# Held-back weight loads, own tiles for w_o_a, an earlier first product, and another planned order in a tuned transformer layer on one Trainium2 core

## The chip, the core and the metric

The kernel runs on one NeuronCore of a Trainium2 chip. Its engines are TensorE (PE in the profile; PEld is its weight load), VectorE (DVE), ScalarE (ACT), GpSimd (POOL) and SyncE (SP). SP issues most DMAs; POOL and ACT can issue some too. The engines run side by side, each through its own list of instructions in order, and wait for each other by semaphores. The metric is the device time of one launch in microseconds. The kernel before took 2119.3 us (median of three runs, 2118.64 to 2120.64).

## The reference

One layer of a decoder trunk on x of 1024 tokens by 1024, all in float32:

```python
x = x + 0.5 * swiglu(rms_norm(x, g_ffn1), w1_gate, w1_up, w1_down)      # hidden 2816
h = rms_norm(x, g_mix)
(c_q, k_a, v_a, k_idx, w_idx, q_b, k_b, v_b, gate_a, gate_b) = split(h @ w_in)
c_q = rms_norm(c_q, g_cq)                                               # 1024 x 256, the "latents"
q_a   = rope(rms_norm(c_q @ w_uq_a, g_q_a));  q_idx = rope(c_q @ w_q_idx)
score = sum over heads of relu(q_idx . k_idx) * w_idx                   # causal; best 256 keys per query
y_a = softmax attention over the selected keys, then w_uv_a             # 1024 x 512
y_b = stick-breaking attention of q_b, k_b, v_b                         # 1024 x 512
merged = sigmoid(gate_a) * (y_a @ w_o_a) + sigmoid(gate_b) * (y_b @ w_o_b)
x = x + merged @ w_out
x = x + 0.5 * swiglu(rms_norm(x, g_ffn2), w2_gate, w2_up, w2_down)
```

## The kernel before

**Precision.** A float32 operand is split into a high part (ACT copies it to fp32r, a matmul type) and a low part (DVE or POOL subtracts the high part). A product is three matmuls, high by high, high by low and low by high. `split` (L297) does this for weights: a load on SP into a raw tile ("woa2r"), the high part on ACT ("woa2h"), the low part on POOL ("woa2l"). Tiles come from pools with a fixed number of buffers. A tile's load waits until the readers of the one that it replaces are done.

**Stages, in order of time.** The first FFN runs until some 656 us. Its gate and up products (`ffn_in`) use a scheme of seven products on 2 x 2 blocks: A11 to A22 are blocks of weights, B11 to B22 blocks of the normed and transposed x, S and T sums of them. At the start the four x tiles are read, ACT sums their squares, POOL takes the root, `norm` (L435) writes both halves of a normed tile on DVE ("ay"), PE transposes it ("pst"), and `turn` (L441) turns the transposes into B's high parts (ACT) and low parts (DVE). The first product is that of A11 and B11 ("pg"). What `ffn_in` makes goes to DRAM ("staged"). `ffn_out` (L715) reads it back ("aS49r", "aA127r") with the down weights ("aw", "ab") in four passes n of eleven steps p, twelve matmuls "p" each.

From some 656 to 1361 us come the projections and both attentions. Their first part makes c_q's rows: `latent_rows` normalizes them ("cqn" from "pscq", L846), POOL stores them to DRAM ("cqd", L1038), and `latents` (L1549) loads them back and PE transposes them ("pscqt", L1562). In this phase the order of PE, DVE, ACT and POOL is fixed by a planner, the class `Weave` (L97). Its parts are generators that name the engine and the tiles they need next; it keeps an estimated clock for each engine, takes the step that can start first, and records it. `cost` estimates an instruction. `flush` (L141) adds it to the clock, with a random factor of 3% either way drawn from a seed (`luck`), and reckons a DMA that POOL or ACT issues at 0.55 or 0.37 us, a constant of 2.4 us and the bytes at 250 GB/s. SP's order comes from the surrounding tile framework.

In this phase: "psdot" are the index scores' dots, "relu" their evacuation by ACT (L1742), "u" the weighted sum on DVE (L1749); "psf" are projections with a high part "evh" (ACT), a low part "evl" (DVE), or, for the gates, "evg" (ACT), which POOL stores in "gd" (L1249) from a ring of three tiles; "qx" and "qy" are turned by PE in "psqt" (L1715); "psz" are stick-breaking logits, "left" their evacuation; "pso" is the attention's sum over values, "yt" its evacuation, "psoa" the first half of y_a @ w_o_a (weights "oa0" to "oa6"), merged with the gates and stored in "md".

From 1361 us on comes the second half of y_a @ w_o_a ("psm", weights "woa0" to "woa6"), which DVE and ACT merge with the gates (loads "gate<-gd", "gate<-obd") into "m". Then comes w_out ("psout", weights "wout000" and so on), and the second FFN with the same functions as the first, until 2118 us. `ring` (L849) gives that stage its tiles for operands and for raw weights, each from two pools in turn. woa0 and woa2 are already fetched while the planner still runs.

The functions that the change touches:

## Time and profile before

| | before |
|---|---|
| median of the runs | 2119.3 us (2118.64 to 2120.64) |
| profiled execution, its own time | 2119.98 us |
| its span | 2118.2 us |
| PE busy | 2099.0 us (99%), 10196 matmuls |
| DVE, ACT, POOL busy | 72%, 50%, 43% |
| DMA | 387.79 MB, mean 183 GB/s |
| granted PE clock | 0.999 |

The page of the profile gives each engine's busy time, and the chain of work that ended last, followed back from the last instruction. A row of a timeline is: start, duration, engine, line of the kernel, operation, output<-input, shape, count; in square brackets the idle time of that engine before it, and what ended it. A row of the waits is: the waiting engine, line and tile, what it waited for, total, number and longest. A row of the DMA view ends with the count, the size of one and the median from issue to landing. A row of the windows is: window and length, busy time and count for PE, PEld, DVE, ACT and POOL, clock, DMA share, GB/s. All are in us.

### The profile page before, as it was taken

What the parts mean: (1) busy time and instruction counts of PE and PEld (TensorE: products, weight loads), DVE (VectorE), ACT (ScalarE), POOL (GpSimd) and SP (SyncE); (2) the same over time, 40 slices, a digit from 0 to 9 for tenths busy, and PEclk for the clock granted to TensorE, in tenths of its full rate; (3) what the DMA queues carried; (4) which work ended last, traced back from release to release, by engine and by line L of the source; (5) the groups of instructions that cost most, each with busy time, mean ns of one, the idle gap of its engine ahead of it and who ended that gap; (6) DMA issues with size and microseconds to landing.
All of it is one profiled execution on the core that took longest, in us unless ns stands there. A gap on an engine that the chain in (4) does not pass through costs nothing.

```text
span 2118.2 us, 29830 instructions
## 1 busy us (share of the span) xinstructions
PE 2099.0 (99%) x10196; PEld 1762.7 (83%) x10196; DVE 1520.3 (72%) x2483; ACT 1058.0 (50%) x1992; POOL 911.2 (43%) x727
## 2 busy tenths in 40 slices
PE   9999999999999999999999999999999999999999
PEld 7888888888889978888888888878888888888887
DVE  7866767678875599788896688865756556487675
ACT  6343343334445356788896687535432322324443
POOL 6654555532336334431213342355655545542233
PEclk9999999999999999999999999999999999999999
DMA  5577777497685253586647754764143333359655
GB/s 150 158 249 220 244 205 236 155 326 255 208 228 159 74 162 110 207 225 171 178 158 232 257 174 157 239 230 157 46 125 100 105 98 126 95 189 335 217 174 189
DMA packets 298104, 387.79 MB, mean 183 GB/s; under 512 B 40144, under 2 KB 186224, under 8 KB 297952
## 3 DMA queue, kind: packets, MB, share of 16 engines
q1 hardware_dynamic: 285088, 343.90, 52.4%
q0 software_dynamic: 12864, 41.99, 5.4%
q8 instruction: 80, 1.31, 0.3%
q14 instruction: 72, 0.59, 0.1%
HBM read 264.67 MB, written 121.15 MB: 182 GB/s over the span
## 4 chain that ended last, share of the span: by engine, by line
PE 90%; DVE 3%; issue 2%; DMA 2%; ACT 2%; POOL 1%; SPq 0%; POOLq 0%; ACTq 0%; DVEq 0%
PE p L778 7%; PE p L779 7%; PE p L777 6%; PE pd L540 4%; PE pd L538 4%; PE pc L538 4%; PE pd L539 4%; PE pa L540 4%; PE pa L538 4%; PE pa L539 3%; PE pc L540 3%; PE pc L539 3%; PE psf L316 3%; PE psf L317 3%; PE psf L318 3%
## 5 line engine op out<-in xcount | busy, mean ns | idle before, releaser
L1390 ACT ACTIVATE junka<-u,cand,sig 128x1024 bf16<-128x1024 f32 (+3 forms) x124 | 134.2, 1082 | 5.7 <-DVE cand L1382 3.7
L1836 DVE TENSOR_TENSOR_SCAN left<-left,hidden 128x640 f32<-128x640 f32 (+3 forms) x64 | 89.1, 1411 | 1.6 <-ACT left L1830 1.4
L901 ACT ACTIVATE swh<-swr 128x512 fp32r<-128x512 f32 x48 | 30.2, 630 | 117.1 <-issue 52.2
L902 DVE TENSOR_TENSOR swr<-swr,swh 128x512 f32<-128x512 f32 x48 | 42.4, 884 | 39.6 <-ACT swh L901 36.9
L1890 DVE SCALAR_TENSOR_TENSOR pt<-pstT,pt 128x512 fp32r<-128x512 f32 (+1 forms) x96 | 51.5, 548 | 18.3 <-ACT pt L1887 17.6
L681 ACT ACTIVATE b0u<-b0u 128x512 f32<-128x512 f32 x20 | 12.6, 632 | 99.8 <-DVE b0u L561 84.4
L1249 POOL DMA_DIRECT2D gd<-evg x32 | 17.9, 560 | 86.8 <-ACT evg L1244 61.5
L1742 ACT ACTIVATE relu<-psdot 128x512 f32<-128x512 f32 (+1 forms) x80 | 40.4, 523 | 29.7 <-DVE u L1749 20.2
L1887 ACT ACTIVATE pt<-pstT 128x512 fp32r<-128x512 f32 (+1 forms) x96 | 46.4, 495 | 17.5 <-PE pstT L1962 14.8
L778 PE MATMUL p<-aT,aS 128*128 128x512 f32 x132 | 51.5, 390 | 1.2 <-DVE aT L391 1.2
L778 PE MATMUL p<-bT,bS 128*128 128x512 f32 x132 | 51.4, 389 | 0.0
L1749 DVE SCALAR_TENSOR_TENSOR u<-relu,WI,u 128x512 f32<-128x512 f32 (+1 forms) x70 | 49.7, 731 | 2.3 <-ACT relu L1742 1.4
L779 PE MATMUL p<-aT,aS 128*128 128x512 f32 x132 | 50.8, 390 | 0.0
L779 PE MATMUL p<-bT,bS 128*128 128x512 f32 x132 | 50.7, 389 | 0.0
L777 PE MATMUL p<-bT,bS 128*128 128x512 f32 x132 | 47.0, 389 | 0.0
L1962 PE MATMUL pstT<-ident,left 128*128 128x128 f32 x288 | 46.0, 273 | 0.0
L2016 ACT ACTIVATE e<-e,mx 128x768 f32<-128x768 f32 (+7 forms) x54 | 41.0, 760 | 8.9 <-DVE mx L2007 8.6
L777 PE MATMUL p<-aT,aS 128*128 128x512 f32 x132 | 44.9, 389 | 0.0
L1830 ACT ACTIVATE left<-psz 128x512 f32<-128x512 f32 (+2 forms) x96 | 43.2, 501 | 2.5 <-PE psz L1855 2.4
L1962 PEld LDWEIGHTS pstT<-ident,left 128*128 128x128 f32 x288 | 35.8, 140 | 8.5
L390 ACT ACTIVATE bT<-bt 128x512 fp32r<-128x512 f32 x44 | 26.2, 624 | 31.8 <-PE p L779 27.6
L1386 DVE TENSOR_SCALAR_CACHE_REDUCE junkv<-u,cand 128x512 uint8<-128x512 f32 (+1 forms) x62 | 41.6, 671 | 0.5
(3065 smaller groups left out, 8130.1 us busy)
## 6 DMA issues: line engine op xcount, KB each, us to landing
aw<-in_w_down_dram SPq DMA_DIRECT2D x33, 512.0 KB, 5.0
bw<-in_w_down_dram SPq DMA_DIRECT2D x33, 512.0 KB, 5.1
swr<-in_w_in_dram SPq DMA_DIRECT2D x48, 256.0 KB, 6.0
a0r<-in_w_gate_dram SPq DMA_DIRECT2D x22, 512.0 KB, 7.9
a1r<-in_w_up_dram SPq DMA_DIRECT2D x22, 512.0 KB, 7.3
b0r<-in_w_gate_dram SPq DMA_DIRECT2D x22, 512.0 KB, 4.3
b1r<-in_w_up_dram SPq DMA_DIRECT2D x22, 512.0 KB, 3.9
x<-in_x_dram SPq DMA_DIRECT2D x16, 512.0 KB, 6.3
```

Source lines behind the costliest of these rows:

```text
L316: nc.tensor.matmul(ps, ah, bh, start=first, stop=False)
L317: nc.tensor.matmul(ps, ah, bl, start=False, stop=False)
L318: nc.tensor.matmul(ps, al, bh, start=False, stop=last)
L538: nc.tensor.matmul(ps, a[:, c], b[k][:, HI], start=start and k == 0, stop=False, skip_group_check=True)
L539: nc.tensor.matmul(ps, a[:, c], b[k][:, LO], start=False, stop=False, skip_group_check=True)
L540: ins = nc.tensor.matmul(ps, a[:, l], b[k][:, HI], start=False, stop=k == 3, skip_group_check=True)
L777: nc.tensor.matmul(ps[q][m], S[:, h], T[:, HI], start=p == 0, stop=False)
L778: nc.tensor.matmul(ps[q][m], S[:, h], T[:, LO], start=False, stop=False)
L779: nc.tensor.matmul(ps[q][m], S[:, l], T[:, HI], start=False, stop=p == last)
L1390: nc.scalar.activation(junks[1][:, 0:(i + 1) * P], score[i], AF.Sign, scale=sig[:, b:b + 1], bias=cand.bitcast(F32)[:, b:b + 1], accum_out ...
L1836: nc.vector.tensor_tensor_scan(back, back, ones, 1.0, op0=ALU.mult, op1=ALU.max)
L1962: nc.tensor.transpose(tp[:, q * P:(q + 1) * P], A[n + q][:, j * P:(j + 1) * P], ident)
```

## The change

1. The start of the first FFN: the second halves of the norms of x tiles 2 and 3 move from DVE to ACT (`norm(late)`, `rest`). The first product (A11 with B11) stands right behind B11's transposes, ahead of B21's, with its matmul on B's low part last in each group of three. The copy of the first raw bank (`also`) goes to the end of `turn`, and B21's banks are named in another order.
2. The loads of the weights for c_q ("wcq0", "wcq1") and for v_b ("wvb00", "wvb01") each wait for a product of the first FFN's last pass (`pace`, `late_in_tail`).
3. c_q's rows are stored by SP where POOL did it, and loaded back in two halves each.
4. The planner reckons a store with a constant of 3.4 us in place of 2.4, and draws its factors from another seed.
5. w_o_a's remaining parts take tiles of the last stage's own pool, and that stage's raw tiles come from its own pool first.

```diff
--- before.py
+++ after.py
@@ -110,7 +110,7 @@
         self.ready, self.done, self.base = defaultdict(float), defaultdict(float), defaultdict(float)
         self.by, self.held, self.marks = {}, defaultdict(int), {}
         self.streams, self.own, self.last = [], None, 0.0
-        self.luck = random.Random(111)
+        self.luck = random.Random(96)
         self.cold, self.shared, self.sbuf, self.summed = 0, [], 0.0, False
 
     def cost(self, i, eng, outs, ins):
@@ -156,7 +156,7 @@
                     t, eng = self.free[SP] + 4.0, "DMA"
                 else:
                     t = max(t, self.free[eng]) + (0.55 if eng == POOL else 0.37)
-                    self.free[eng], t, eng = t, t + 2.4 + mb / 0.25, "DMA"
+                    self.free[eng], t, eng = t, t + 3.4 + mb / 0.25, "DMA"
             else:
                 cost, late = self.cost(i, eng, outs, ins)
                 cost *= self.luck.uniform(1 - 0.03, 1 + 0.03) if eng != PE else 1.0
@@ -294,11 +294,11 @@
         nc.gpsimd.tensor_tensor(rs, ms, mhalf[:, 0:n], op=ALU.pow)
         return rs
 
-    def split(src, nm, view, rawt=rawt, wt=wt):
+    def split(src, nm, view, rawt=rawt, wt=wt, pace=lambda i: i):
 
         raw = rawt(nm + "r")
         rv, n = view(raw)
-        nc.sync.dma_start(rv, src)
+        pace(nc.sync.dma_start(rv, src))
         wh = wt(nm + "h")
         nc.scalar.activation(wh[:, 0:n], raw[:, 0:n], AF.Copy)
         wl = wt(nm + "l")
@@ -402,7 +402,7 @@
         def __init__(self, g, bank, gains, yt, ct, tt, ts, spare, nm):
             self.g, self.bank, self.gains, self.yt, self.ct = g, bank, gains, yt, ct
             self.tt, self.ts, self.spare, self.nm = tt, ts, spare, nm
-            self.B, self.y, self.gcol = {}, {}, None
+            self.B, self.y, self.gcol, self.late = {}, {}, None, []
 
         def busy(self, n):
 
@@ -432,10 +432,17 @@
             nc.scalar.activation(j.bitcast(BF16), self.x[t], AF.Square, accum_out=ss)
             self.rs[t] = rsqrt(ss, 1, D)
 
-        def norm(self, t):
+        def norm(self, t, late=False):
             xt = self.x[t]
-            for c, out_ in ((slice(0, 1024), xt),) if self.half else ((HI, self.y[0, 0][t]), (LO, self.y[0, 1][t])):
+            for c, out_ in ((slice(0, 1024), xt),) if self.half else ((HI, self.y[0, 0][t]), (LO, self.y[0, 1][t]))[:1 if late else 2]:
                 nc.vector.tensor_scalar(out_, xt[:, c], self.rs[t], None, op0=ALU.mult)
+            if late:
+                self.late.append((self.y[0, 1][t], xt[:, LO], self.rs[t]))
+
+        def rest(self):
+
+            out_, x_, rs = self.late.pop(0)
+            nc.scalar.activation(out_, x_, AF.Copy, scale=rs)
 
         def operands(self, *ns):
             for n in ns:
@@ -457,11 +464,11 @@
                 t = self.B[n][k]
                 self.keep([(t[:, HI], ps)])
                 self.less([t[:, LO]], [ps], [f32(t[:, HI])])
-                if also is not None and not k:
-                    self.keep([(also, ps)], nc.vector)
                 if less:
                     self.less(less[0][k:k + 1], [ps], less[1][k:k + 1])
                 out.append(ps)
+            if also is not None:
+                self.keep([(also, out[0])], nc.vector)
             return out
 
         def keep(self, copies, eng=None):
@@ -532,12 +539,14 @@
 
             return rest if early else rest()
 
-        def times(a, b, ps, start=True):
+        def times(a, b, ps, start=True, low_last=False):
             for k in range(4):
                 c, l = slice(k * P, (k + 1) * P), slice(512 + k * P, 512 + (k + 1) * P)
-                nc.tensor.matmul(ps, a[:, c], b[k][:, HI], start=start and k == 0, stop=False, skip_group_check=True)
-                nc.tensor.matmul(ps, a[:, c], b[k][:, LO], start=False, stop=False, skip_group_check=True)
-                ins = nc.tensor.matmul(ps, a[:, l], b[k][:, HI], start=False, stop=k == 3, skip_group_check=True)
+                sides = [(a[:, c], b[k][:, HI]), (a[:, c], b[k][:, LO]), (a[:, l], b[k][:, HI])]
+                if low_last:
+                    sides[1:] = sides[:0:-1]
+                for n, (x_, y_) in enumerate(sides):
+                    ins = nc.tensor.matmul(ps, x_, y_, start=start and not k and not n, stop=k == 3 and n == 2, skip_group_check=True)
             return ins
 
         def mul(O, n, ps, start=True):
@@ -580,11 +589,11 @@
 
             ps, sg = {}, {}
 
-            def half(r, c, q, letter=None):
+            def half(r, c, q, letter=None, low_last=False):
 
                 if not q:
                     ps[r, c] = bank("pg", letter)
-                times(O[0][f"A{r + 1}{q + 1}"], B[f"B{q + 1}{c + 1}"], ps[r, c], not q)
+                times(O[0][f"A{r + 1}{q + 1}"], B[f"B{q + 1}{c + 1}"], ps[r, c], not q, low_last)
 
             def gate(r, c):
                 sg[r, c] = ct(f"{nm}sg")
@@ -596,11 +605,14 @@
 
             if "B11" not in B:
                 left(0, "A11")
+                R.rest()
                 R.operands("B12", "B11", "B21", "B22", "T1")
                 R.kept()
                 copies = list(zip(R.raw["T3"], R.turn("B11", between=6, also=R.raw["T3"][0])))
+                half(0, 0, 0, "a", True)
+                R.rest()
                 left(0, "A12")
-                p21 = R.turn("B21")
+                p21 = R.turn("B21", "bcda")
                 R.kept2()
                 copies += zip(R.raw["T4"], p21)
                 left(0, "A21", "A22")
@@ -623,7 +635,8 @@
             A[1].update(S)
             for t in rows:
                 R.norm(t)
-            half(0, 0, 0, "a")
+            if (0, 0) not in ps:
+                half(0, 0, 0, "a")
             half(0, 0, 1)
             gate(0, 0)
             left(1, "S2")
@@ -712,6 +725,8 @@
 
     STAGED = {n: i for i, n in enumerate(("A11", "A12", "A22", "S1", "S2", "S3", "S4"))}
 
+    product_of = {}
+
     def ffn_out(nm, xs, wd, raw, op, sums, aux, bank, staged, after):
 
 
@@ -776,7 +791,7 @@
                         h, l = slice(m * P, (m + 1) * P), slice(512 + m * P, 512 + (m + 1) * P)
                         nc.tensor.matmul(ps[q][m], S[:, h], T[:, HI], start=p == 0, stop=False)
                         nc.tensor.matmul(ps[q][m], S[:, h], T[:, LO], start=False, stop=False)
-                        nc.tensor.matmul(ps[q][m], S[:, l], T[:, HI], start=False, stop=p == last)
+                        product_of[nm, n, p] = nc.tensor.matmul(ps[q][m], S[:, l], T[:, HI], start=False, stop=p == last)
 
                 for _ in range(2):
                     if later:
@@ -846,10 +861,11 @@
         nc.vector.tensor_scalar(c, ps, rs, None, op0=ALU.mult)
 
 
-    def ring(pool):
+    def ring(pool, own=False):
 
         op = in_turn((wt, 4), (lambda name: pool.tile([P, 1024], F32R, tag="r", name=name, bufs=NR), NR))
-        raw = in_turn((rawt, 2), (lambda name: pool.tile([P, 1024], F32, tag="raw", name=name, bufs=2), 2))
+        raws = [(rawt, 2), (lambda name: pool.tile([P, 1024], F32, tag="raw", name=name, bufs=2), 2)]
+        raw = in_turn(*(raws[::-1] if own else raws))
         return op, raw
 
     def of(pool, tag, bufs, n=1024, dt=F32):
@@ -926,7 +942,7 @@
             for t in range(4):
                 if t < 3:
                     R.stat(t + 1)
-                R.norm(t)
+                R.norm(t, t > 1)
             R.second = lambda: R.place(xs[4:8], 1, sums)
             ffn_in("a", R, w1_gate, w1_up, raw, op, sums, ct, bank, staged[0], range(4), first, beside)
             assert not agenda and not held and not halved and not pieces
@@ -1019,9 +1035,12 @@
         aux = of(pool, "u", 8, 512)
         sums = in_turn((sums, 5), (lambda name: f32(pair(name)), 2))
         ffn_out("a", xs, w1_down, raw, op, sums, aux, bank, staged[0], after)
-        Wcq = [wcols(w_in, C_CQ, QR, 4 * j, 4, f"wcq{j}", rawt=raw,
+        def late_in_tail(p):
+            return lambda load: behind(product_of["a", 3, p], load)
+
+        Wcq = [wcols(w_in, C_CQ, QR, 4 * j, 4, f"wcq{j}", rawt=raw, pace=late_in_tail(j),
                      wt=lambda name: rpool.tile([P, 1024], F32R, tag="r", name=name, bufs=NR)) for j in range(2)]
-        Wvb = [wcols(w_in, C_VB, 256, 4 * j, 4, f"wvb0{j}") for j in range(2)]
+        Wvb = [wcols(w_in, C_VB, 256, 4 * j, 4, f"wvb0{j}", pace=late_in_tail(2 + j)) for j in range(2)]
 
         Rka, Rwi = [rawt(f"wka{j}r") for j in range(2)], cst.tile([P, 8 * ND], F32, name="wir")
         for j in range(2):
@@ -1035,7 +1054,7 @@
                 c = lat(f"cqn{half}{q}")
                 for j in range(2):
                     latents_normed(c[:, j * QR:(j + 1) * QR], banks_(q + j))
-                put_low(cqd[half][:, q * QR:(q + 2) * QR], c)
+                nc.sync.dma_start(cqd[half][:, q * QR:(q + 2) * QR], c)
 
         def one(q):
             ps = bank("pscq")[:, 0:QR]
@@ -1550,7 +1569,8 @@
 
             rows = [sring(f"cqn{half}") for half in range(2)]
             for half in (1, 0):
-                nc.sync.dma_start(rows[half], cqd[half])
+                for c in (slice(0, 512), slice(512, 1024)):
+                    nc.sync.dma_start(rows[half][:, c], cqd[half][:, c])
                 nc.sync.dma_start(*((rope, roped), (ropeq, ropeqd))[1 - half])
             for half in (1, 0):
                 cqn, outs = rows[half], []
@@ -2258,12 +2278,13 @@
 
 
     with ctxf, tc.tile_pool(name="ring2", bufs=1) as rpool, tc.tile_pool(name="ps6", bufs=1, space=PSUM) as psum:
-        op, raw = ring(rpool)
+        op, raw = ring(rpool, True)
         bank = banks(psum, fpsum)
         with tc.tile_pool(name="m0", bufs=1) as mpool:
             M0 = []
             for d in range(0, ND, 2):
-                wh, wl = first.pop(0) if first else wcols(w_o_a, d * P, 2 * P, 0, 4, f"woa{d}")
+                wh, wl = first.pop(0) if first else wcols(w_o_a, d * P, 2 * P, 0, 4, f"woa{d}",
+                                                              wt=lambda name: rpool.tile([P, 1024], F32R, tag="r", name=name, bufs=NR))
                 for e in range(2):
                     r = slice((d + e) * P, (d + e + 1) * P)
                     g = ht("gate", F32)
```

Where instructions move, the orders of the two kernels show it. First PE at the start: "pst" are transposes (of "ay" with numbers 244 to 247 for B11, 248 to 251 for B21), "pg" the first product. Before:

```order
L452 MATMUL pst_353<-ident_71,ay02_246 128x128
L452 MATMUL pst_353<-ident_71,ay03_247 128x128
L452 MATMUL pst_363<-ident_71,ay10_248 128x128
L452 MATMUL pst_363<-ident_71,ay11_249 128x128
```

...and twelve more transposes later:

```order
L452 MATMUL pst_384<-ident_71,ay13_251 128x128
L538 MATMUL pg_456<-aB110_293,a00A11_286 128x512
L539 MATMUL pg_456<-aB110_293,a00A11_286 128x512
```

Now:

```order
L459 MATMUL pst_351<-ident_71,ay02_246 128x128
L459 MATMUL pst_351<-ident_71,ay03_247 128x128
L549 MATMUL pg_359<-aB110_292,a00A11_284 128x512 x3
L549 MATMUL pg_359<-aB111_293,a00A11_284 128x512 x3
L549 MATMUL pg_359<-aB112_294,a00A11_284 128x512 x3
L549 MATMUL pg_359<-aB113_295,a00A11_284 128x512 x3
L459 MATMUL pst_376<-ident_71,ay10_248 128x128
L459 MATMUL pst_376<-ident_71,ay11_249 128x128
```

The first product stands behind the last of B11's transposes, and B21's sixteen follow it.

Second, ACT around the split of the weight wvb11 at some 822 us, in the planned part. Before:

```order
L1742 ACTIVATE relu<-psdot 128x384
L1742 ACTIVATE relu<-psdot 128x512
L1742 ACTIVATE relu<-psdot 128x384
L1128 ACTIVATE wvb11h<-wvb11r 128x1024
L1225 ACTIVATE evh<-psf 128x512
L1742 ACTIVATE relu<-psdot 128x512
L1742 ACTIVATE relu<-psdot 128x384
```

Now:

```order
L1762 ACTIVATE relu<-psdot 128x384
L1762 ACTIVATE relu<-psdot 128x512
L1762 ACTIVATE relu<-psdot 128x384
L1762 ACTIVATE relu<-psdot 128x512
L1147 ACTIVATE wvb11h<-wvb11r 128x1024
L1244 ACTIVATE evh<-psf 128x512
L1744 ACTIVATE qsa<-psqt 64x4x128
L1762 ACTIVATE relu<-psdot 128x384
L1762 ACTIVATE relu<-psdot 128x512
```

wvb11h still stands between relus, with evh behind it, and now a qsa as well.

Third, SP at the end of the attention, where the loads for the merged half stand ("gate" are the gates' rows and the stored products). Before:

```order
L1124 DMA woa2r<-in_w_o_a_dram 128x4x256
L2185 DMA both<-gd 128x512
L2188 DMA both<-obd 128x512
L2185 DMA both<-gd 128x512
L2188 DMA both<-obd 128x512
L301 DMA woa4r<-in_w_o_a_dram 128x4x256
L2270 DMA gate<-gd 128x512
L2271 DMA gate<-obd 128x512
```

Now, after ten other loads of "gate":

```order
L2291 DMA gate<-gd 128x512
L2292 DMA gate<-obd 128x512
L1143 DMA woa2r<-in_w_o_a_dram 128x4x256
L2291 DMA gate<-gd 128x512
L2292 DMA gate<-obd 128x512
L2291 DMA gate<-gd 128x512
L2292 DMA gate<-obd 128x512
L301 DMA woa4r<-in_w_o_a_dram 128x4x256
L301 DMA woa6r<-in_w_o_a_dram 128x4x256
L301 DMA wout000r<-in_w_out_dram 128x2x512
```

woa2r stood ahead of all loads of "gate", and stands behind twelve of the sixteen; the other weights stand behind all of them.

## The prediction

> **What bounds the kernel now.** I read the page first: busy time by engine, then the chain that ended last.
>
> ```profile
> PE 2099.0 (99%) x10196; PEld 1762.7 (83%) x10196; DVE 1520.3 (72%) x2483; ACT 1058.0 (50%) x1992; POOL 911.2 (43%) x727
> PE 90%; DVE 3%; issue 2%; DMA 2%; ACT 2%; POOL 1%; SPq 0%; POOLq 0%; ACTq 0%; DVEq 0%
> ```
>
> TensorE (PE) is busy in 2099.0 of 2118.2 us and is 90% of the chain. The change neither adds nor removes a matmul, so only PE's idle time can change. Where that lies, by stage (length after the colon, then PE's busy time and matmuls; the last columns are granted clock, DMA share, GB/s):
>
> ```profile
> 725.00:1361.00 636.00, 630.77 (x3393) 536.80 (x3391) 528.63 (x1175) 470.78 (x952) 208.38 (x250) 1.00 0.60 183
> 1361.00:1480.00 119.00, 116.51 (x523) 95.35 (x524) 69.06 (x80) 50.72 (x75) 59.10 (x32) 1.00 0.60 213
> 1480.00:2118.00 638.00, 633.56 (x2807) 523.86 (x2805) 411.56 (x522) 226.76 (x401) 293.40 (x198) 1.00 0.46 150
> ```
>
> The last stage gives a matmul's price: 633.56 / 2807 = 0.226 us. It also holds the tail after the last matmul, some 4 us, which the change leaves alone. The clock is full in all three. So the question is which of PE's waits go, and the waits of PE, summed by what ended them (us in total, times, longest), are the list to work through:
>
> ```profile
> PE psdot L1771 <- ACT relu L1742: 2.6, 4, 1.4
> PE psout L317 <- POOL wout000l L305: 1.2, 1, 1.2
> PE p L778 <- DVE aT L391: 1.2, 1, 1.2
> PE pscqt L1562 <- DMA cqn<-cqd: 1.2, 1, 1.2
> PE psf L316 <- ACT evg L1244: 1.2, 1, 1.2
> PE pst L452 <- ACT ay L432: 0.9, 1, 0.9
> PE pst L452 <- DVE ay L438: 0.8, 2, 0.7
> PE psqt L1715 <- POOL qx L1707: 0.7, 1, 0.7
> PE psz L1854 <- ACT left L1830: 0.6, 2, 0.3
> PE psm L316 <- DVE yt L1909: 0.6, 1, 0.6
> PE psm L318 <- POOL woa6l L305: 0.6, 1, 0.6
> PE psm L316 <- ACT woa2h L1128: 0.2, 1, 0.2
> ```
>
> These sum to 11.6 us, and each touches a part of the change. That is the ceiling of any gain here, 0.55%.
>
> **The start.** Two of the eight norm halves leave VectorE (DVE), and the first product moves ahead of B21's sixteen transposes. A row of DVE (tile 2) and one of ScalarE (ACT):
>
> ```profile
> 9.71 0.88 DVE L438 TENSOR_SCALAR ay<-x,rs 128x512 f32<-128x512 f32 x2 [0.66 <-POOL rs L294]
> 12.30 2.42 ACT L473 ACTIVATE aB<-pst,agcol 128x512 fp32r<-128x512 f32 x4 [0.81 <-PE pst L452]
> ```
>
> Only tiles 2 and 3 lose their second half (0.44 us each). Tile 2's comes off ahead of tile 3's statistic, so the last x tile is normed some 0.3 us sooner: a gain of 0.3 in the wait on ay (0.8). Against it stands the cover. Before, B21's sixteen transposes ran while ACT and DVE turned B11 into high and low parts. Now the product follows at once, and needs the first block's low part: ACT 0.6 (2.42 / 4) after the transposes, then one DVE step of 0.74 at most, against four blocks' transposes of about 0.4 each and two matmuls that don't read it. That leaves some 0.2 us of wait there, and some 0.4 at B21, whose transposes now end just ahead of their product. Sum +0.3. Bounds: -0.3 if all is hidden, +0.8 if each of the two waits lasts a whole ACT step.
>
> **Weight loads held back.** Here SyncE's queue (SP), the ACT step that waited, and PE:
>
> ```profile
> 595.27 0.38 SPq L301 DMA_DIRECT2D wcq0r<-in_w_in_dram  x1
> 600.78 1.14 SPq L301 DMA_DIRECT2D wcq1r<-in_w_in_dram  x1
> 602.01 0.53 SPq L722 DMA_DIRECT2D aS310r<-staged  x1
> 612.98 0.63 ACT L390 ACTIVATE aS<-aS310r 128x512 fp32r<-128x512 f32 x1 [6.41 <-DMA aS310r<-staged]
> 617.89 0.50 PE L778 MATMUL p<-aT,aS 128*128 128x512 f32 x1 [1.23 <-DVE aT L391]
> 648.16 1.07 ACT L303 ACTIVATE wcq0h<-wcq0r 128x1024 fp32r<-128x1024 f32 x1
> ```
>
> aS310r is 256 KB and took 11 us to land, issued right behind two 512 KB weight loads that aren't used for another 50 us. ACT stood 6.4 us for it, and PE then 1.23. With both loads gone from ahead of it, even half of those 6.4 us covers 1.23: -1.2. The loads move behind ab_5863, each after a product of the last pass (wcq0r first, wvb00r two places on). An estimate for wcq0r: its product ends 27 us (ten products of twelve matmuls) before the pass does at 656, so it goes out near 629, and even at aS310r's 11 us it lands 8 us ahead of its split at 648.16. Nothing that stands behind them on SP is wanted sooner than its own buffer comes free. Bounds: -1.2 and 0 (DMA contention has another source).
>
> **The latents' rows.** GpSimd (POOL) stored them and SP loaded them back:
>
> ```profile
> 685.91 0.54 POOL L1038 DMA_DIRECT2D cqd<-cqn  x1 [0.27 <-DVE cqn L846]
> 691.68 0.32 SPq L1553 DMA_DIRECT2D cqn<-cqd  x1
> 695.37 0.85 PE L1562 MATMUL pscqt<-ident,cqn 128*128 128x128 f32 x6 [1.19 <-DMA cqn<-cqd]
> staged<-b0u SPq DMA_DIRECT2D x20, 256.0 KB, 2.2
> x2d<-x SPq DMA_DIRECT2D x16, 256.0 KB, 3.7
> ```
>
> The path is store 5.8 us, load 3.7, wait 1.19. SP's stores of the same 256 KB land in 2.2 to 3.7, so 2.1 us or more come off against 1.19 to save: -1.2. SP now issues four stores and four half loads in place of two loads, six more of some 0.35 us. The pair of cqd0 waits for DVE at 685.6, and behind it stand only the rows themselves and weights issued after 691.68 before. Bounds: -1.2 and 0. [...]
>
> **The planner.** The scatter's seed and one us more for a listed store change no work, but they reorder all five engines from some 725 to 1361 us, where PE loses 2.6 + 1.2 + 0.7 + 0.6 = 5.1 us by the rows above. I went through those places in the new order:
>
> ```profile
> 822.03 1.06 ACT L1128 ACTIVATE wvb11h<-wvb11r 128x1024 fp32r<-128x1024 f32 x1 [1.61 <-PE psf L317]
> 808.00:826.00 18.00, 16.14 (x77) 13.04 (x75) 17.29 (x33) 10.43 (x21) 9.24 (x10) 1.00 0.34 118
> 1146.26 0.60 ACT L1244 ACTIVATE evg<-psf 128x512 f32<-128x512 f32 x1 [1.42 <-DMA gd<-evg]
> gd<-evg POOLq DMA_DIRECT2D x32, 256.0 KB, 5.0
> ```
>
> The longest wait on relu (1.4) comes of wvb11h: it waits on ACT for PE to leave the weight's slot, and the relus stand behind it. The new order keeps wvb11h behind four relus with evh behind it: 1.4 stays. Of the other relu waits (2.6 - 1.4 = 1.2) the later ones have some 0.7 us (three matmuls) more cover and go; 0.4 stays. psqt on qx gets four matmuls more (+0.9 of cover), and loses two list steps of DVE ahead of qy (1.0): 0.9. psz keeps its form: 0.6. The third evg stood 1.42 us on ACT until a gate store landed and freed its buffer; the planner now reckons 0.55 + 3.4 + 1.05 = 5.0 us for such a store, which is the row's median, where it took 4.0, and at one of the two places where it is close psf's pairs lie farther apart: 0.6 of 1.2 stays. Sum 3.9 of 5.1: -1.2. What I can't see is where the new order has a wait of its own, so this term is the wide one: -4 (four fifths of the 5.1 gone) to +3 (two more places like the worst two, 1.4 + 1.2, and a bit).
>
> **The merged half.** w_o_a's parts now come from the pool's own slots, so a split needn't wait for PE to leave an older one:
>
> ```profile
> 1353.54 0.50 SPq L2270 DMA_DIRECT2D gate<-gd  x1
> 1360.98 0.32 SPq L2271 DMA_DIRECT2D gate<-obd  x1
> 1359.91 1.06 ACT L1128 ACTIVATE woa2h<-woa2r 128x1024 fp32r<-128x1024 f32 x1 [0.54 <-issue]
> 1361.06 2.70 POOL L1133 TENSOR_TENSOR woa2l<-woa2r,woa2h 128x1024 fp32r<-128x1024 f32 x1 [2.40 <-ACT woa2h L1128]
> 1363.78 0.38 SPq L301 DMA_DIRECT2D woa6r<-in_w_o_a_dram  x1
> ```
>
> Before, PE lost 0.2 (woa2h) + 0.6 (yt) + 0.6 (woa6l) + 1.2 (wout000l) = 2.6. In the new order the attention's last matmuls lie ahead of 48 of psoa (10.8 us), so yt is early; and wout000 is split without waiting for woa's slots. But woa2r now stands behind twelve gate loads on SP. Those took 1353.54 to 1361.3, 7.8 us. Counted from psoa's 48, woa2h is wanted after 72 matmuls, 16.3 us, and its low part 0.9 later. The gate loads start a few us ahead of that count; woa2r goes out 6 to 8 us into it, lands 6 later, and with 1.06 and 2.70 is split at 16 to 18. woa6r waits for woa2l's end, and woa6h is wanted 6.3 us after woa2h. So 0 to 1 at each, and I take 0.9 in all for 2.6: -1.7. Bounds: -2.6 and +1.
>
> **The sum.** +0.3 - 1.2 - 1.2 - 1.2 - 1.7 = -5.0. The profiled execution took 2119.98 (1.8 beside its span of 2118.2), 0.7 above the median of 2119.3, so 2115.0 on its scale and **2114.3** on the median's.
>
> **Rivals.** Below, "same" is within 0.2% (4.2 us), about what a measurement of this kernel tells from no change.
>
> First, the new order's own waits eat the gain. For it: DVE was busy 17.29 of 18 us around 808 to 826, where two of the relu waits lie, so a few list steps put early make PE wait; against it: over the whole stage DVE has 107 us to spare. Planner term +3, total -0.8: 2118.5.
>
> Second, w_o_a comes late. SP's order speaks for it (a load behind twelve others); 10.8 us of psoa ahead of it speak against. If woa2r goes out 3 us later, woa2l and woa6h cost 3 in all in place of 0.9, and the start's +0.8 may join: 2117.
>
> Third, SP's store is as slow as POOL's, and the held loads were not what aS310r waited for: both terms 0, so 2116.7. Against it, the two loads stand right ahead of aS310r.
>
> Fourth, slower: DVE becomes the bound in the list stage. There the steps on relu take 0.73 each, against three matmuls' 0.68:
>
> ```profile
> L1749 DVE SCALAR_TENSOR_TENSOR u<-relu,WI,u 128x512 f32<-128x512 f32 (+1 forms) x70 | 49.7, 731 | 2.3 <-ACT relu L1742 1.4
> ```
>
> In one stretch of the new order, 38 matmuls (8.6 us) stand beside DVE steps that I count at 12.8; before, that stretch was even. If PE has no lead there, that place costs up to 4.2 us. With one such place the total is about zero (4.2 against the other terms' -3.8); it decides from the second on, 8.4 - 3.8 = +4.6, so 2123.9.
>
> Fifth, the planner's order happens to free most of the 5.1: term -4, 2111.5.
>
> **How the numbers follow.** The forecast 54% (its own range 2112 to 2116.5), the first rival 17%, the second 10%, the third 3%, the fourth 7%, the fifth 9%. The likeliest is 2114.3. Faster than 2115.1 are the fifth and most of the forecast's share (46 of 54): 55%. Slower than 2123.5 is the fourth: 7%. The rest, 38%, is within 0.2%. The range takes in the first three rivals and part of the fifth: 2110.5 to 2119.5.
>
> **What would show it.** In the profile after: no wait of p on aT near 618, and ACT's wait for aS310r under 3 us; cqd's stores landing in under 4 us and no wait of pscqt; at the start, pg waiting on aB for 0.2 and 0.4; wvb11h still ahead of a wait of psdot; no psm on yt, and a wait on woa2l or woa6h below 1 each. A PE sum between 725 and 1361 us more than 3 above 5.1, or any wait over 2 us there, would make the prediction wrong, and so would a matmul price other than 0.226.

## The result: slower by 0.69%

| | before | changed |
|---|---|---|
| median of six runs | 2119.97 us (2118.64 to 2120.85) | 2133.84 us (2132.49 to 2137.20) |
| ratio | | 1.0069, 95% interval 1.0056 to 1.0081 |
| profiled execution, its span | 2119.98, 2118.2 us | 2132.49, 2130.7 us |

The change cost 13.9 us, where a gain of 5.0 had been forecast. The profiled execution of the changed kernel is the fastest of its six. It has the same 10196 matmuls, and PE is again the chain. The largest waits of PE, summed by what ended them:

```profile
PE pst L363 <- DVE mlo L372: 5.5, 2, 4.6
PE psdot L1791 <- ACT relu L1762: 3.5, 4, 1.6
PE pst L459 <- ACT ay L432: 2.0, 2, 1.2
PE psm L316 <- ACT woa4h L303: 1.6, 1, 1.6
PE pa L549 <- DVE ar L478: 1.4, 1, 1.4
PE psz L1874 <- ACT left L1850: 1.4, 2, 1.0
...
PE psm L318 <- POOL woa2l L1152: 1.3, 1, 1.3
PE pscqt L1582 <- DMA cqn<-cqd: 1.1, 3, 0.5
...
PE psm L316 <- ACT woa2h L1147: 0.7, 1, 0.7
...
PE psm L318 <- POOL woa4l L305: 0.5, 1, 0.5
```

Of the waits that the change was to remove, those on aT (1.2), evg (1.2), qx (0.7), yt, woa6l and wout000l are gone. In their place stand others in the same stages, and the largest, 5.5 us on mlo (the low part of the normed and transposed rows that the projections use), had no counterpart before. Since PE's work is the same, the start of the matmul with a given number in PE's order, in the one trace less in the other, shows where the time went:

| matmuls | stage | the changed kernel falls behind by |
|---|---|---|
| up to 203 | start of the first FFN | 2.3 us |
| to 2854 | down products, place of the old wait on aT | -1.5 |
| to 2956 | end of the first FFN, 645 to 671 us | 9.0 |
| to 3466 | c_q's rows loaded back | 0.4 |
| to 7136 | planned stage and merged half | 2.5 |
| to the end | w_out, second FFN | -0.3 |

Before rounding, the rows sum to the 12.5 us between the two spans; the medians differ by 1.4 more.

**The largest piece.** SP's issues of the changed kernel, from its timeline, then the answers for three tiles (duration of the issue in ns, start; then the time from issue to landing in us):

```profile
630.09 0.38 SPq L301 DMA_DIRECT2D wcq0r<-in_w_in_dram  x1
630.57 0.46 SPq L1019 DMA_DIRECT2D xd<-x  x1
631.12 0.38 SPq L737 DMA_DIRECT2D aA127r<-staged  x1
631.59 0.43 SPq L301 DMA_DIRECT2D wcq1r<-in_w_in_dram  x1
632.12 2.08 SPq L775 DMA_DIRECT2D ab<-in_w_down_dram  x2
634.29 0.59 SPq L737 DMA_DIRECT2D aA128r<-staged  x1
634.97 0.56 SPq L301 DMA_DIRECT2D wvb00r<-in_w_in_dram  x1
...
L301 SPq DMA_DIRECT2D wcq0r<-in_w_in_dram x1: 384/384/384, 630.1 to 630.1; - x1
DMA to landing us min/median/max: 10.4/10.4/10.4
...
L737 SPq DMA_DIRECT2D aA127r<-staged x1: 382/382/382, 631.1 to 631.1; - x1
DMA to landing us min/median/max: 11.3/11.3/11.3
...
L737 SPq DMA_DIRECT2D aA128r<-staged x1: 593/593/593, 634.3 to 634.3; - x1
DMA to landing us min/median/max: 14.9/14.9/14.9
```

wcq0r landed at 640.5, and aA127r, half its size and issued 1 us later, at 642.4. SP's landings stand here in the order of issue: the last load ahead of wcq0r at 632.5, wcq0r 8.0 us after it, a store of x 1.3 after that, and then aA127r. aA128r behind wcq1r landed at 649.2; before it took 3.5 us. The same happened to aS310r near 602 us in the kernel before, which took 10.9; here there is less slack. Then ACT, and PE:

```profile
642.55 0.63 ACT L390 ACTIVATE aA<-aA127r 128x512 fp32r<-128x512 f32 x1 [9.42 <-DMA aA127r<-staged]
...
649.24 0.63 ACT L390 ACTIVATE aA<-aA128r 128x512 fp32r<-128x512 f32 x1 [0.65 <-DMA aA128r<-staged]
...
650.29 0.67 ACT L371 ACTIVATE mhi<-pst,gcolm 128x512 fp32r<-128x512 f32 x1
...
652.53 0.66 PE L363 MATMUL pst<-ident,m1xn 128*128 128x128 f32 x4 [4.60 <-DVE mlo L372]
655.39 0.63 PE L793 MATMUL p<-aB,aA 128*128 128x512 f32 x1
655.82 0.63 PE L794 MATMUL p<-aB,aA 128*128 128x512 f32 x1
...
640.00:650.00 10.00, 7.86 (x42) 6.10 (x40) 2.05 (x2) 2.54 (x5) 1.29 (x2) 1.00 0.98 240
650.00:656.00 6.00, 2.61 (x11) 2.18 (x12) 4.53 (x5) 4.96 (x9) 4.44 (x4) 0.76 0.15 56
656.00:662.00 6.00, 6.00 (x24) 4.80 (x23) 3.23 (x5) 3.71 (x6) 3.64 (x2) 0.67 0.46 69
```

In ACT's list the evacuation of the transposed m1xn (650.29) stands behind aA127r and aA128r (642.55 and 649.24), and PE stood 4.6 us for it (mlo is what DVE makes of mhi). Then the windows' clock column falls to 0.76 and 0.67: a matmul's step is 0.43 us (655.39 to 655.82), and 0.23 again from 661.13 to 661.36. Of the row's 9.0 us, 5.5 are waits, 2.8 were lost from 654.05 to 660.03 with the clock at half, and 0.7 at restarts and a short stop ahead of them.

**The start.** Here the product of the up weights waits for DVE, which copies B21's transposes out of PSUM:

```profile
24.68 0.74 DVE L478 TENSOR_SCALAR ar<-pst,agcol 128x512 f32<-128x512 f32 x1
...
25.57 2.99 PE L549 MATMUL pa<-aB,a10A 128*128 128x512 f32 x12 [1.36 <-DVE ar L478]
```

Of the 2.3 us, 1.6 come up here, with the restart. The longer waits on ay cost little: where the first product begins, the changed kernel is 0.2 behind, and ahead of the place above 0.7.

**c_q's rows.** SP's stores were issued at 695.42 behind wqir, and the loads that need them at 702.24; the wait of pscqt went from 1.2 to 1.1 in all:

```profile
694.89 0.43 SPq L1143 DMA_DIRECT2D wqir<-in_w_q_idx_dram  x1
695.42 0.89 SPq L1057 DMA_DIRECT2D cqd<-cqn  x2
702.24 1.25 SPq L1573 DMA_DIRECT2D cqn<-cqd  x2
```

**The merged half.** woa2r was issued after twelve gate loads and landed 8.0 us later, and its split and those behind it were late in a row. woa4r had landed at 1381.41, but its split began only when a store of md had landed, at 1385.98:

```profile
1369.29 0.42 SPq L1143 DMA_DIRECT2D woa2r<-in_w_o_a_dram  x1
...
1377.40 1.06 ACT L1147 ACTIVATE woa2h<-woa2r 128x1024 fp32r<-128x1024 f32 x1 [9.51 <-DMA woa2r<-in_w_o_a_dram]
...
1386.24 1.06 ACT L303 ACTIVATE woa4h<-woa4r 128x1024 fp32r<-128x1024 f32 x1 [0.60 <-DMA md<-o]
```

### The profile page after: what moved, and what is told of

It reads as the page before. It is cut to its first block, busy times and chain, and to the rows that moved or that the text cites. A ratio compares the mean times of both kernels' runs of the same rounds, so it can differ in the third digit from the quotient of the medians.

```text
span 2130.7 us, 29881 instructions
## 1 busy us (share of the span) xinstructions
PE 2102.3 (99%) x10196; PEld 1763.1 (83%) x10196; DVE 1521.9 (71%) x2483; ACT 1058.0 (50%) x1992; POOL 912.6 (43%) x727
## 4 chain that ended last, share of the span: by engine, by line
PE 88%; DVE 5%; DMA 3%; issue 2%; ACT 1%; POOL 1%; SPq 0%; POOLq 0%; DVEq 0%; ACTq 0%
PE pd L549 10%; PE pa L549 10%; PE pc L549 10%; PE p L794 6%; PE p L792 6%; PE p L793 6%; PE pb L549 5%; PE psf L316 3%; PE psf L317 3%; PE psf L318 3%; PE pg L549 2%; PE pstT L1982 1%; PE pso L2138 1%; PE psout L316 1%; PE psout L317 1%
## 5 line engine op out<-in xcount | busy, mean ns | idle before, releaser
L1409 ACT ACTIVATE junka<-u,cand,sig 128x640 bf16<-128x640 f32 (+3 forms) x124 | 134.6, 1085 | 2.6 <-DVE cand L1401 1.5
L2036 ACT ACTIVATE e<-e,mx 128x768 f32<-128x768 f32 (+7 forms) x54 | 41.0, 759 | 11.6 <-DVE mx L2027 11.3
L2218 POOL TENSOR_TENSOR o<-o,gate 128x512 f32<-128x512 f32 x16 | 23.1, 1445 | 47.6 <-ACT o L2213 47.6
```

Of the source, the lines that this page charges most:

```text
L1409: nc.scalar.activation(junks[1][:, 0:(i + 1) * P], score[i], AF.Sign, scale=sig[:, b:b + 1], bias=cand.bitcast(F32)[:, b:b + 1], accum_out ...
```

## Experiments

Each time below is told as its difference from the kernel before on the same chip, since that kernel's own median lay between 2119.3 and 2121.2 in these comparisons. The changed kernel's is +13.9.

**One part undone at a time.** The held loads:

```diff
-        Wcq = [wcols(..., rawt=raw, pace=late_in_tail(j), wt=...) for j in range(2)]
-        Wvb = [wcols(w_in, C_VB, 256, 4 * j, 4, f"wvb0{j}", pace=late_in_tail(2 + j)) for j in range(2)]
+        Wcq = [wcols(..., rawt=raw, wt=...) for j in range(2)]
+        Wvb = [wcols(w_in, C_VB, 256, 4 * j, 4, f"wvb0{j}") for j in range(2)]
```

> The changed kernel with its second part undone: the loads of the weights wcq0, wcq1 and wvb00 stand again where the kernel before has them. Theory: three weight loads of 512 KB, issued within 5 us of each other, held up the loads of aA127r and aA128r behind them on SP's queue, and the idle stretch of 4.6 us that PE spent on that brought its clock down to half for some 6 us. Then the stage from 640 to 665 us loses its 9.0 us of delay, the old wait of 1.2 us near 618 us returns, and the time falls by about 7.5 to 2126.3. Rival: the stage is late because the start is 2.3 us late and everything behind it shifted against the loads; then the time falls by less than 3, to 2131 or more.

Measured +9.1 (2129.23; ratio 1.0040, 1.0025 to 1.0055): 4.8 less than the changed kernel, less than the 7.5 that I expected. In its trace the stage between matmul 2854 and 2956 loses 0.0 in place of 9.0, and the wait on aT is back with 0.8. So the place is right. The trace shows what took part of the gain: where two waits on relu follow each other, the clock falls here, and does not in the changed kernel's profile. The window right behind the same two waits (1.29 and 1.55 us in both), in this kernel and then in the changed one:

```profile
830.00:834.00 4.00, 3.38 (x15) 3.38 (x16) 3.83 (x10) 3.14 (x6) 0.54 (x1) 0.59 0.74 261
```

```profile
836.00:840.00 4.00, 3.76 (x28) 3.70 (x29) 3.81 (x11) 3.01 (x7) 0.54 (x1) 1.00 0.83 259
```

That stretch costs 1.5 us, and a like one at the start (clock 0.63 between 6 and 14 us) 1.3. They come in some executions and not in others: of the five traces with this planned order (this one, the changed kernel and the runs with the start, w_o_a's tiles and the banks undone), three have the one at the relu waits. So medians of a few runs compare to 1 or 2 us only, and a part's price is better read from the stage in the trace.

The start:

```diff
+                if also is not None and not k:
+                    self.keep([(also, ps)], nc.vector)
...
-            if also is not None:
-                self.keep([(also, out[0])], nc.vector)
...
-                R.rest()
...
-                half(0, 0, 0, "a", True)
-                R.rest()
                 left(0, "A12")
-                p21 = R.turn("B21", "bcda")
+                p21 = R.turn("B21")
...
-                R.norm(t, t > 1)
+                R.norm(t)
```

> The changed kernel with its first part undone: all norms on DVE, the first product behind B21's transposes. Theory: the first part alone made PE 2.3 us late by 35 us (1.4 us of it a product that waits for DVE to clear a PSUM bank, some 0.4 an x tile that landed late in the profiled run), so the time falls by 1.9 to 2.3, to about 2131.7, and PE's wait of pa on ar is gone. Rival: the 2.3 us are made up for later, because the kernel waits for loads further on; then the time is the same within 0.5.

Measured +11.5 (2131.66; 1.0049, 1.0033 to 1.0066), 2.4 less than the changed kernel. At matmul 203 it is 0.4 behind the kernel before in place of 2.3, and the wait on ar is gone. The theory holds; nothing is made up for later.

The planner:

```diff
-        self.luck = random.Random(96)
+        self.luck = random.Random(111)
...
-                    self.free[eng], t, eng = t, t + 3.4 + mb / 0.25, "DMA"
+                    self.free[eng], t, eng = t, t + 2.4 + mb / 0.25, "DMA"
```

> The changed kernel with the planner as before: the old seed, a store at 2.4 us. Theory: between 725 us and 1361 us the two orders lose nearly the same (5.1 and 5.6 us of waits), but the new order puts the load of woa2 behind twelve gate loads, which cost the merged half 4.1 us of waits against 2.6. So the time falls by 0.5 to 2.5, to between 2131.3 and 2133.3. Rival: w_o_a's own tiles are what delays the merged half; then PE's waits of psm there stay at some 4 us and the time falls by 1 at most.

Measured +5.2 (2125.37; 1.0023, 1.0014 to 1.0032), 8.7 less than the changed kernel: far more than expected. In its trace, from matmul 3466 to 7136, it gains 3.5 on the kernel before, where the changed kernel loses 2.5. psm now waits 0.8 in all where it was 4.1, and neither woa4 nor woa6 nor wout000 is late any more:

```profile
PE psm L316 <- DVE yt L1929: 0.6, 1, 0.6
...
PE psm L316 <- ACT woa2h L1147: 0.2, 1, 0.2
```

So own tiles for w_o_a do what they were to do, in the old order, and the rival falls. That leaves 2.7 of the 8.7 which the two traces don't show. The changed kernel's 2.5 is the least of the five traces with its planned order: the other four lose 2.7, 4.5, 5.3 and 5.5 in this stretch, with stretches at half clock behind the two relu waits (three of them) or near 925 and 1382 us (the one with the start undone, whose granted clock is 0.996 over the span), and 0.2 to 0.8 more on psz. So undoing it gives between 6.0 and 8.9 by the traces, and the 8.7 lies within.

w_o_a's tiles:

```diff
-        op, raw = ring(rpool, True)
+        op, raw = ring(rpool)
...
-                wh, wl = first.pop(0) if first else wcols(..., f"woa{d}", wt=lambda name: rpool.tile(...))
+                wh, wl = first.pop(0) if first else wcols(..., f"woa{d}")
```

> The changed kernel with its fifth part undone: woa4 and woa6 take the shared tiles, and raw tiles come from the shared pool first. Theory: woa2r's place on SP is the planner's and stays, so psm's waits on woa2h and woa2l (2.0 us) stay, and woa4 and woa6 wait in addition for PE to leave older tiles: slower than the changed kernel by 0.5 to 2, some 2135. Rival: the own tiles are what delays woa4 and woa6 (their memory comes free only late); then the time falls by 1 to 2, to about 2132.

Measured +11.8 (2131.98; 1.0054, 1.0039 to 1.0069), 2.1 less than the changed kernel, as the rival had it: the waits on woa2h and woa2l stay (0.7 and 1.3), and those on woa4 are gone. woa4r goes out 4.6 us behind woa2r and lands 12.1 us after woa2r's issue in both kernels. What differs is the split: 1.2 us after the landing here (1385.15 to 1386.38), and 4.8 in the changed kernel, where it waits for a store of md. That the own tile's memory is what this store still reads is the likely reason, but no row shows it. So own tiles help in the one order and hurt in the other.

**The parts on the kernel before.** c_q's rows by SP, in halves, with the next weight's load put behind them:

```diff
-                put_low(cqd[half][:, q * QR:(q + 2) * QR], c)
+                nc.sync.dma_start(cqd[half][:, q * QR:(q + 2) * QR], c)
...
+                if nm == "wqi":
+                    tc.add_manual_dep(load.ins, here["rows"].ins.name, ...NoSync...)
```

> The kernel before with the third part alone (c_q's rows stored by SP, loaded in halves), and in addition the load of wqir, 512 KB, put behind the rows' last loads on SP where it stood ahead of their store. Theory: a transfer lands in the order of issue on SP's queue, so it was wqir ahead of the store, and not the engine that issues it, that made the store take 5.7 us in the kernel before and 6.7 in the changed one. Then the store of cqd0 lands within 3.5 us of its issue, PE's wait of pscqt (1.2) goes, and the time falls by 1 to 1.3, to 2119. Rival: the store is slow to DRAM whatever stands ahead; then it still takes over 5 us, pscqt still waits for about 1, and the time is the same within 0.3.

Measured -2.2 (2117.11; 0.9989, 0.9980 to 0.9998), and no wait of pscqt is left. SP's timeline:

```profile
684.67 0.92 SPq L1038 DMA_DIRECT2D cqd<-cqn  x2
688.82 0.98 SPq L1557 DMA_DIRECT2D cqn<-cqd  x2
689.85 0.42 SPq L1124 DMA_DIRECT2D wqir<-in_w_q_idx_dram  x1
```

The loads go out 4.2 us after the stores, where it was 5.8 in the kernel before and 6.8 in the changed one. The held loads are not the reason: with them put back in the changed kernel, stores and loads are still 6.9 apart, and pscqt waits 2.0. So it is wqir's place. No run keeps POOL's stores with wqir behind them, so what SP alone gives against POOL is not separated. (The stage's gain in the trace is 1.4; the other 0.8 of the median lies elsewhere or is chance.)

w_o_a's own tiles alone, the edit of the diff's last hunks:

> The kernel before with the fifth part alone (w_o_a's own tiles, own raw tiles first). Theory: with the old order of SP, where woa2 and woa4 stand ahead of the gate loads, the own tiles take away the waits on woa6l and wout000l (1.8 by the rows, 2.1 with the restarts), so the time falls by 2 to 2.3, to about 2118; what made the merged half slower in the changed kernel was the planner's order. Rival: own tiles come free too late in any order; then the waits of psm and psout stay at 2.6 or more, and the time doesn't fall.

Measured -1.6 (2117.65; 0.9992, 0.9983 to 1.0001); the interval still holds 1, but in the trace the merged half gains 2.3, and the waits on woa6l and wout000l are gone (only yt 0.6 and woa2h 0.2 are left). The theory holds.

One held load, wcq1, behind the last staged load:

```diff
+        def late_in_tail(j):
+            return (lambda load: behind(product_of["a", 3, 5], load)) if j else (lambda load: load)
...
```

> The kernel before with only the load of wcq1 held back, until the sixth product of the last pass, which puts it behind the last staged load aA1210r; wcq0 and wvb00 stay. Theory: each weight load occupies SP's queue for 5 to 8 us, and what counts is which loads stand behind it. Behind wcq1 there is now no load that the down products need, and aS310r lands some 5.6 us sooner. Then the wait on aT near 618 us (1.2) goes, no wait comes up between 640 and 665 us, and the time falls by 1 to 1.5, to 2118.8. Rival: holding a load is bad as such, because its split comes late on ACT and POOL; then a wait on mlo or on wcq1's parts of 1 us or more comes up, and the time doesn't fall.

Measured -1.3 (2118.01; 0.9994, 0.9985 to 1.0003), again with 1 in the interval. In the trace the wait on aT near 618 us is gone, its place gains 1.5 (up to matmul 2854 the trace gains 0.7, since 0.8 are lost near 487 and 497 us, long ahead of the held load), and mlo has no wait. ACT waited 0.79 for aS310r, where it was 6.41:

```profile
608.16 0.63 ACT L390 ACTIVATE aS<-aS310r 128x512 fp32r<-128x512 f32 x1 [0.79 <-DMA aS310r<-staged]
```

The three together:

> The three edits of the runs before together on the kernel before: rows by SP with wqir behind them, own tiles for w_o_a, and only wcq1 held. Theory: the gains lie in three stages that don't touch, so they add: -1.2, -2.1 and -1.4, about -4.7, to 2115.4. Rival: a wait saved early is lost again at a later wait for a load, so the sum is under half of that, 2118 or more.

Measured -5.5 (2113.79, 2113.19 to 2116.21; ratio 0.9973, 0.9962 to 0.9983): faster than both kernels, and about the sum of the three (-5.1 by their own runs). Its profiled execution is the slowest of the eight and lost 2.2 at the start, with the clock at half from 13.0 to 16.4 us (0.999 over the span); the three stages gain 1.5, 1.4 and 2.9 in it.

**The planner's two halves, alone on the kernel before.** Only the store's cost, then only the seed:

```diff
-                    self.free[eng], t, eng = t, t + 2.4 + mb / 0.25, "DMA"
+                    self.free[eng], t, eng = t, t + 3.4 + mb / 0.25, "DMA"
```

> The kernel before with one half of the fourth part: a listed store is reckoned with 3.4 us, the seed stays. The planner gives another order from 730 us on, but woa2 still stands ahead of the gate loads. Theory: the order of the planned stage is a matter of chance and moves its waits by 2 us or so either way, and the merged half stays as it was; so the time is within 2.5 of the kernel before, and the wait of psf on evg (1.2) is gone or under 0.6, since stores are reckoned as long as they take. Rival: reckoning stores longer is what made the planned stage slower; then the time rises by 3 or more.

```diff
-        self.luck = random.Random(111)
+        self.luck = random.Random(96)
```

> The kernel before with the other half of the fourth part: the new seed, a store at 2.4 us. Here too woa2 stands ahead of the gate loads. Theory: only both together gave the order in which woa2 is behind twelve gate loads; with the seed alone the time is within 2.5 of the kernel before, and psm's waits on woa2 stay under 0.5. Rival: the seed alone brings the 3 to 6 us that the planner's part cost the changed kernel.

Neither theory held: +11.3 (2132.50; 1.0052, 1.0038 to 1.0067) and +11.2 (2132.32; 1.0052, 1.0037 to 1.0067). The first lies in its rival's range (3 or more), the second beyond both. The waits on evg did go in both. But each order has new ones, elsewhere. Of the first:

```profile
PE psz L1854 <- ACT left L1830: 4.5, 2, 2.9
PE pspT L2141 <- ACT e L2026: 3.2, 1, 3.2
...
PE pspT L2141 <- DVE moree L2028: 1.4, 1, 1.4
...
PE psm L318 <- POOL woa6l L305: 1.2, 1, 1.2
```

Of the second:

```profile
PE pspT L2141 <- DVE e L2028: 4.1, 2, 3.7
PE psdot L1771 <- ACT relu L1742: 2.7, 3, 1.9
PE psz L1854 <- ACT left L1830: 2.6, 2, 1.5
```

Each has one wait of over 3 us for the softmax of an attention tile near 1235 us, with a stretch of lower clock beside it. So it is neither the seed nor the cost by itself: of the four pairs, old with old and new with new give the two better orders (against the kernel before, the stage and the merged half lose 13.0, 11.4 and, new with new, 2.5 in the traces). Another draw of the random factors of 3% alone moves this stage by 11 us.

**PSUM banks at the start.** The changed kernel with one argument undone:

```diff
-                p21 = R.turn("B21", "bcda")
+                p21 = R.turn("B21")
```

> The changed kernel with one word of its first part undone: B21's transposes take the PSUM banks in the order a, b, c, d and not b, c, d, a. Theory: the product pa of the up weights takes bank a; with B21's last transposes in it, pa waits for the last of DVE's copies of the transposes (ar). With the first ones in it, that copy is done 2 us sooner, the wait of pa on ar (1.4) goes, and at most 0.4 comes up ahead of B21's first transpose: the time falls by 1 to 1.4, to about 2132.6. Rival: pa waits for a10A's parts or for all of DVE's list, whichever bank it takes; then the wait stays within 0.3.

Measured +10.2 (2131.38; 1.0044, 1.0027 to 1.0060), 3.7 less than the changed kernel. The wait of pa on ar (1.4) is gone from the trace, and no wait ahead of B21's transposes took its place. In this trace the start is still 2.2 us behind at matmul 203, since the clock was at half there from 8.1 to 15.0 us (0.91 over the first 36). The runs with the loads and with w_o_a's tiles undone have the same stretch and the changed kernel's banks, and are 3.6 and 3.8 behind: the banks cost some 1.5. The rest of the median's 3.7 is not shown; such stretches, which come and go, are a likely cause.

**The held loads alone on the kernel before**, all three as in the changed kernel:

> The kernel before with the second part alone: wcq0, wcq1 and wvb00 held to the first three products of the last pass, as in the changed kernel. Taking this part out of the changed kernel gave 4.6 us by the medians, while its trace shows 7.5 for the stage. Theory: the part itself costs 6 to 7.5 (5.5 us of waits and some 2.5 us at half clock, less the 1.5 near 618), and the smaller difference of the medians came of half-clock stretches elsewhere (the start, the two relu waits), which hit some executions and not others. Then this kernel takes 2126 to 2127, the clock is at half for some 6 us after a wait of over 4 us near 652. Rival: the part costs 4.6 on its own, 2124.5 or less, because the stall is shorter where the start is not late.

Measured +6.7 (2127.69; 1.0031, 1.0020 to 1.0042); in the trace the end of the first FFN loses 8.8, after a gain of 1.5 at the old wait on aT. Its windows:

```profile
640.00:650.00 10.00, 6.07 (x31) 4.75 (x29) 3.84 (x4) 3.51 (x6) 2.56 (x2) 1.00 0.91 236
650.00:656.00 6.00, 4.27 (x15) 3.46 (x16) 3.96 (x5) 5.67 (x9) 4.86 (x3) 0.61 0.01 3
656.00:662.00 6.00, 6.00 (x28) 4.94 (x27) 2.82 (x4) 2.56 (x5) 2.80 (x2) 0.82 0.52 90
```

The stall and the half clock are there with an undisturbed start. The theory's 6 to 7.5 holds.

## Why the prediction was wrong

Two terms turned the sign, the held loads (+6.7 alone) and the new planned order (8.7 when undone); the others missed by some 3 us or less each.

- **What bounds the kernel** was right: PE and its waits. (The twelve rows shown add up to 11.8 as printed, not 11.6.) But "the ceiling of any gain" says nothing of a loss, and each part was priced by the waits that it would remove.
- **The start, +0.3 forecast, 2.3 measured.** The transposes' cover was weighed, and ahead of the wait on ar the start lost 0.7, near the forecast. The failing step is that the banks' other order was costed at nothing. With B21's last transposes in bank a, the up product waits for the last of DVE's copies: 1.4, and 1.6 with the restart (the run with the banks in the old order has no such wait).
- **The held loads, -1.2 forecast, +6.7 alone.** The removed wait was right (-1.5 in the traces). The step that failed is "Nothing that stands behind them on SP is wanted sooner than its own buffer comes free". I asked when the held loads themselves are needed, and they were in time; what now stood behind them was not. The row for it was in the prediction: aS310r took 11 us behind two such loads, and the same 11 us came to aA127r and 15 to aA128r. The half clock then added 2.8 that I had not thought of.
- **c_q's rows, -1.2 forecast, about 0.** The failing step took SP's landing times from other stages, and of those the short ones (2.2 to 3.7): the same view of the kernel before has SP's stores of 256 KB at up to 8.1 (staged<-a0c). In this stage the stores land behind wqir. The trace of before held the sign: wqir was issued 1.4 us ahead of POOL's first store and landed 0.7 ahead of it (690.3 and 691.0), though SP issued the one and POOL the other. The third rival had this half right and its other half, the held loads, wrong.
- **The planner, -1.2 forecast.** Undone, with the merged half that depends on it, it gives 8.7, of which the first two traces show 6.0. Going through the places of the old waits was the mistake in kind: evg and qx did go, as said, but an order's cost lies in its new places, and its waits by rows are 5.6 us where I had 3.9. The first rival named this and priced it at 3.
- **The merged half, -1.7 forecast, +1.5 by the rows (4.1 against 2.6).** The second rival had the place and one cause, woa2r behind the gate loads, and 3 for it. woa2r did go out some 8 us after psoa's last 48 matmuls began, within the forecast; the mis-sized step is its load, which took 8.0 us where 6 were assumed (issue 1369.29, split from 1377.40): 2.0 of the 4.1. The other 2.1 are waits on woa4, in the new order a cost of the own tiles themselves, which the term counted only as a gain.
- **The slower rival** had 7%. It named another mechanism, DVE as the bound of the list stage. That is seen at one place, and smaller than the 4.2 given for it: at the second of the two relu waits (1.55) ACT stood for DVE's u, and DVE was busy from 830 to 836 us without a break.

```profile
835.59 0.60 ACT L1762 ACTIVATE relu<-psdot 128x512 f32<-128x512 f32 x1 [1.69 <-DVE u L1769]
```

Over the whole stage the waits on relu rose by 0.9 only. Five terms, four of them of an unknown sign, should not have had so narrow a range.

## What to carry to other kernels

When a load is moved on a queue, price what stands behind it in its new place before what it frees in its old one: here wcq0r and wcq1r landed 8.0 and 4.7 us after what stood ahead of them, and aA128r behind both took 14.9 us where it had taken 3.5. When a planner's order is drawn anew, don't expect the cost of the order that is given up: the three other draws seen here cost this stage 2.5 to 13 us more in their traces. Measure the order apart from the other edits. A part that is right can be hidden by one that is wrong: three of these five gave 5.5 us together on the old order, two of them altered (wqir behind the rows, and one held load in place of three).

## What the runs showed of the hardware

In these runs a wait of PE could cost more than its length. After the 4.6 us the granted clock was at half from 653.1 to 660.0 (0.51 over that window), 2.8 us of extra time; with the held loads alone on the kernel before, after a wait of 4.3 us, it was 0.61 from 650 to 656 us and 0.82 from 656 to 662. In the five traces with the changed kernel's planned order, two waits of about 1.3 and 1.6 us that lie close together had a stretch at half clock behind them in three (0.59 over 4 us with the loads undone, 0.62 over 4 us with w_o_a's tiles undone, 0.97 over 50 us with the banks undone) and none in two. No run shows what decides between the two.

A load of 512 KB from w_in, in pieces of 1 KB, landed 8.0 us after the load ahead of it on SP's queue (wcq0r, 632.5 to 640.5) or 4.7 us after it (wcq1r, 642.5 to 647.2); a 512 KB store of x behind wcq0r landed 1.3 us after that.
